# First input stage as half-product quads, and the first blocks' mixers moved beside a three-pass second input stage

## The chip, the cores and the metric

The kernel runs on one core of a Trainium2 chip, with the engines PE (matrix products), DVE (vector), ACT (scalar activation), POOL (general) and SP (which here only issues transfers). The metric is the device time of one execution in microseconds. The kernel before the change takes 2793.22 us (median of three runs, 2793.16 to 2797.24).

## The reference

One layer of an encoder on x of 2048 tokens and width 1024, in float32. The parts that matter here:

```python
xn = rms_norm(x, mix_norm_g)
proj = xn @ w_in          # q k v (512 each) | mq mk mv mo (512 each) | i f (4 each) | ga gm (1024 each)
att = chunk_band_attention(aq, ak, av, rel_bias)       # own chunk of 64 and the 8 before it, 8 heads of 64
mqk = silu(causal_depthwise_conv([mq, mk], conv_w, conv_b))            # 4 taps
hm = mlstm_chunkwise(mq_c, mk_c, mv, i, f)             # recurrence over chunks, 4 heads of 128
mlstm_out = sigmoid(mo) * rms_norm(hm, mh_norm_g)
y = sigmoid(ga) * (att @ w_att_proj) + sigmoid(gm) * (mlstm_out @ w_mlstm_proj)
x = x + y @ w_out
x = x + square(relu(rms_norm(x, ffn_norm_g) @ w_up)) @ w_down
return rms_norm(x, final_norm_g)
```

## The kernel before

**Tiles.** The tokens are cut into four blocks of 512; two blocks form a *span* (blocks 0 and 1, blocks 2 and 3). Every float32 operand of a large product is split into a high and a low part (`split`: a cast on ACT, the difference on DVE), and each product of tiles is three matmuls of 128x512: high by high, high by low, low by high. Weights arrive as raw 128x1024 tiles in four buffers `wraw`, are split into three buffers `wsp`, and one such tile feeds 24 matmuls in most stages. The operands live in 28 buffers `r` of 128x2x512. There are 16 buffers `ctx` and 6 `tmp` for 128x512 results, and 8 PSUM banks.

**Half-product quads.** A *quad* (`quad`, L594) multiplies both blocks of a span at once with 256 columns of the output, split in halves of the inner dimension, with seven products in the place of eight, from sums of quadrants of weights and of operands. It costs 7 weight tiles, 168 matmuls. The sums of x (`take_parts`, L1769) give 28 split operands. The sums of weights are made either beside an earlier stage and kept in DRAM (`sum_w`, L400; `wsum`), or when the quad loads its four raw quadrants (`quad_w`, L476). Seven products make four results; `combine` (L1829) copies three of them out of PSUM on ACT (L1840) and adds others on DVE (L1848), for each of two column groups: six copies and six sums a quad. `quad_tok` (L623) does the same for v and mv of the far span.

**The order of stages** is the body of `dense` (L677), the one thread that uses weights, in the order that `weights` (L344) lists them:

1. For block 0 and then block 1: v and mv as token tiles (`token_tiles`), 20 *feature tiles* (`feature_tile`, L535: q, k, mq, mk, mo) and 8 for the gate ga. They are plain products, 24 matmuls each. q and k go from PSUM straight into head operands (`evac_q`, `evac_k`), mq and mk through the convolution (`evac_conv`), and the block's mixers, attention (`attention`, `head`) and recurrence (`recurrence`, `rec_head`), run beside them and leave eight `r` buffers `mix`. Then the two mixer projections of the block, 16 `pair_tile` column groups, go to DRAM (`projd`).
2. The gate stage: two quads for gm of the first span; `after_gate` reads the projections back, applies the gates and writes y. Then two quads of the output projection (`after_out`).
3. The second input stage: 11 items (`IN_ORDER`: nine quads, and v/mv twice) for blocks 2 and 3. Everything is kept in DRAM.
4. Eight up-projection quads of the first span; then the down projection with the mixers of blocks 2 and 3 beside it, their inputs read from DRAM (`attention_far`, `recurrence_far`) and their projections (`project`, L799) at fixed places (`PROJ`).
5. Output, up and down of the second span, and the final norm.

**What sets the order.** `Flow` (L96) runs all threads against written-out costs of each engine and of SP, and issues each instruction on the engine that is free first, by priority; `dense` has the lowest claim on PE but its work is always there. The result is a fixed order of instructions on every engine and of transfers on SP's queue. An engine, and the SP queue, executes its list in order and stops at a wait.

## Time and profile before

| | |
|---|---|
| median of 3 runs | 2793.22 us |
| profiled execution, span from first to last instruction (no other time of it is on record) | 2794.2 us |
| PE busy | 2772.3 us (99%) |
| weight loads of PE (beside PE) | 2300.6 us (82%) |
| DVE busy | 2067.3 us (74%) |
| ACT busy | 1560.8 us (56%) |
| POOL busy | 50.4 us (2%) |
| moved by DMA | 619.31 MB, 222 GB/s over the span |
| mean granted PE clock | 0.999 |

"Busy" is the union of an engine's instructions. Matmuls overlap in the pipeline: the mean duration of one is 390 ns, while one starts every 227 ns or so, and short waits between them are hidden in "busy". The DMA share is the mean busy share of the core's 16 DMA engines. In a group's row stand the line and engine, output and inputs by the program's names, the shape, the count, busy time and mean of one, and then the idle time of the engine just before, with what ended it. The line numbers are those of the kernel before; the changed kernel's lines differ.

### The profile page before, as it was taken

How to read it: one execution, taken by the hardware profiler on the slowest of the kernel's cores; microseconds unless marked ns; L12 is line 12 of the kernel's file. 1: busy time of each engine (PE TensorE's matmuls, PEld its weight loads, DVE VectorE, ACT ScalarE, POOL GpSimd, SP SyncE). 2: the span in 40 equal slices, each digit the busy share in tenths (PEclk: the TensorE clock that was granted, in tenths of full speed). 3: DMA queues.
4: the chain of work that ended last, by engine and by line, in shares of the span. 5: the costliest groups of instructions: out<-in, count | busy, mean ns of one | idle time of the engine just before them, and what ended most of it. 6: DMA issues, size and time to landing. Idle time of an engine off the chain costs nothing.

```text
span 2794.2 us, 38148 instructions
## 1 busy us (share of the span) xinstructions
PE 2772.3 (99%) x13084; PEld 2300.6 (82%) x13084; DVE 2067.3 (74%) x3724; ACT 1560.8 (56%) x2707; POOL 50.4 (2%) x116
## 2 busy tenths in 40 slices
PE   9999999999999999999999999999999999999998
PEld 7888888888878888878888888888888888888887
DVE  7886489968995876876776788789886554457675
ACT  5674366845453544585555677476544665555453
POOL 0000000000000000000000000000000000000000
PEclk9999999999999999999999999999999999999999
DMA  6326743366845798667888876867777575678773
GB/s 223 103 90 198 275 145 97 118 200 230 265 168 198 237 314 283 210 197 261 304 298 281 273 237 209 258 210 226 233 267 232 170 259 203 210 266 274 271 246 129
DMA packets 283921, 619.31 MB, mean 222 GB/s; under 512 B 31568, under 2 KB 46544, under 8 KB 283728
## 3 DMA queue, kind: packets, MB, share of 16 engines
q1 hardware_dynamic: 283584, 616.88, 66.5%
q8 instruction: 102, 1.67, 0.2%
q14 instruction: 91, 0.75, 0.1%
q10 hardware_dynamic: 144, 0.01, 0.0%
HBM read 437.46 MB, written 179.31 MB: 221 GB/s over the span
## 4 chain that ended last, share of the span: by engine, by line
PE 84%; DVE 7%; DMA 3%; issue 3%; ACT 2%; POOL 0%; SPq 0%; POOLq 0%; ACTq 0%; DVEq 0%
PE bank L616 36%; PE bank L532 12%; PE bank L531 12%; PE bank L533 12%; PE bank L644 3%; PE bank L1272 2%; PE bank L1310 2%; PE bank L1341 2%; DVE wsp L472 2%; DMA r<-u 1%; ACT wsp L470 1%; DVE sc L1316 1%; DVE r L1020 1%; PE bank L1636 0%; DMA ctx<-x 0%
## 5 line engine op out<-in xcount | busy, mean ns | idle before, releaser
L616 PE MATMUL bank<-r,wsp 128*128 128x512 f32 x5208 | 1188.2, 390 | 2.2 <-DVE r L1020 1.0
L616 PEld LDWEIGHTS bank<-r,wsp 128*128 128x128 f32 x5208 | 976.3, 188 | 209.7 <-DVE r L1020 2.0
L472 DVE TENSOR_TENSOR wsp<-wraw,wsp 128x1024 fp32r<-128x1024 f32 x460 | 561.9, 1222 | 312.8 <-ACT wsp L470 308.6
L470 ACT CAST wsp<-wraw 128x1024 fp32r<-128x1024 f32 x460 | 483.7, 1052 | 502.5 <-PE bank L616 236.1
L531 PE MATMUL bank<-r,wsp 128*128 128x512 f32 x1600 | 635.4, 397 | 0.6 <-ACT r L1292 0.5
L532 PE MATMUL bank<-r,wsp 128*128 128x512 f32 x1600 | 624.8, 391 | 0.2 <-DVE r L1294 0.2
L533 PE MATMUL bank<-r,wsp 128*128 128x512 f32 x1600 | 624.4, 390 | 0.0
L533 PEld LDWEIGHTS bank<-r,wsp 128*128 128x128 f32 x1600 | 300.4, 188 | 64.3
L531 PEld LDWEIGHTS bank<-r,wsp 128*128 128x128 f32 x1600 | 300.7, 188 | 57.8 <-ACT r L1292 1.3
L532 PEld LDWEIGHTS bank<-r,wsp 128*128 128x128 f32 x1600 | 301.0, 188 | 55.6 <-DVE r L1294 0.8
L1020 DVE TENSOR_TENSOR r<-r 128x512 fp32r<-128x512 f32 x224 | 147.9, 686 | 60.9 <-ACT r L1015 60.1
L1848 DVE TENSOR_TENSOR ctx<-bank,ctx 128x512 f32<-128x512 f32 x174 | 119.1, 688 | 98.3 <-PE bank L616 97.8
L1015 ACT CAST r<-r 128x512 fp32r<-128x512 f32 x224 | 134.4, 622 | 91.1 <-DMA r<-u 88.6
L1840 ACT COPY ctx<-bank 128x512 f32<-128x512 f32 x174 | 100.9, 582 | 74.0 <-PE bank L616 65.7
L1322 ACT ACTIVATE sc<-sc,scs 128x640 f32<-128x640 f32 (+4 forms) x128 | 97.5, 762 | 59.6 <-DVE scs L1316 58.0
L2200 ACT ACTIVATE ctx<-ctx 128x512 f32<-128x512 f32 x96 | 60.6, 632 | 82.8 <-DVE ctx L1848 82.8
L1346 DVE TENSOR_TENSOR r<-bank,r 128x512 fp32r<-128x512 f32 (+1 forms) x168 | 98.0, 594 | 5.3 <-ACT r L1344 3.8
L1272 PE MATMUL bank<-r,r 128*128 128x512 f32 x336 | 96.8, 370 | 2.2 <-DVE r L1346 1.4
L1344 ACT CAST r<-bank 128x512 fp32r<-128x512 f32 (+1 forms) x168 | 81.8, 515 | 18.6 <-PE bank L1341 17.7
L1310 PE MATMUL bank<-r,r 128*128 128x320 f32 (+3 forms) x480 | 85.6, 305 | 0.1
L1341 PE MATMUL bank<-const,sc 128*128 128x128 f32 x560 | 80.1, 273 | 4.7 <-DVE sc L1327 2.0
L415 DVE TENSOR_TENSOR ctx<-ctx,ctx 128x512 f32<-128x512 f32 x112 | 76.3, 686 | 11.1 <-DMA wsum<-ctx 9.6
(285 smaller groups left out, 2898.7 us busy)
## 6 DMA issues: line engine op xcount, KB each, us to landing
wraw<-in_wf SPq DMA_DIRECT2D x170, 512.0 KB, 4.3
wraw<-wsum SPq DMA_DIRECT2D x136, 512.0 KB, 4.2
r<-u SPq DMA_DIRECT2D x224, 256.0 KB, 4.5
wraw<-in_w SPq DMA_DIRECT2D x103, 512.0 KB, 3.6
u<-ctx SPq DMA_DIRECT2D x128, 256.0 KB, 2.4
ctx<-in_wf SPq DMA_DIRECT2D x112, 256.0 KB, 4.1
wsum<-ctx SPq DMA_DIRECT2D x112, 256.0 KB, 3.6
u<-tmp SPq DMA_DIRECT2D x96, 256.0 KB, 3.3
```

The lines of the kernel that those rows point to most:

```text
L470: nc.scalar.copy(w[:, 0], raw)
L472: nc.vector.tensor_sub(w[:, 1], raw, w[:, 0].bitcast(F32))
L531: mm(ps, lh, rh, start=first, stop=False)
L532: mm(ps, lh, rl, start=False, stop=False)
L533: mm(ps, ll, rh, start=False, stop=last)
L616: mm(ps, wv[:, x, k, n], a[:, y], start=new and k == 0 and x == y == 0, stop=k == 3 and x == 1, skip_group_check=True)
L1015: self.nc.scalar.copy(dst[:, 0], src)
L1020: self.nc.vector.tensor_sub(dst[:, 1], src, dst[:, 0].bitcast(F32))
L1272: nc.tensor.matmul(bkv[:, :, c0:c0 + w], st, sl[:, :, o:o + w], start=n == 0, stop=n == total - 1)
L1310: nc.tensor.matmul(bks[x][:, :w], q[:, y, i * P:(i + 1) * P], kf[:, f * P + x * w:f * P + x * w + w], start=y == 0, stop=y == 1)
L1341: nc.tensor.transpose(bk[:, o:o + P], prob[i][0][:, c:c + P], self.ident)
L1848: nc.vector.tensor_add(t[:, o:o + 512], ps, t[:, o:o + 512])
```

## The change

Five things change together.

- **First input stage.** The feature tiles, the gate stage and its two quads go. `dense` first runs v and mv of blocks 0 and 1 as token tiles, and then nine quads (`IN_FIRST`: gm0, q, mq, ga0, k, mk, gm1, mo, ga1) for blocks 0 and 1, from the summed x of both. Their results go to DRAM in the form that blocks 2 and 3 already had. `norm_in` of block 1 runs beside that of block 0.
- **Sums of the second span's x.** They are made beside the first stage and kept in DRAM (`take_x1`, `xud`): 28 tiles.
- **Second input stage in three passes** (`in_far`, `BATCHES`): pass one takes products 0, 3, 1 of all 11 items, pass two 2 and 4, pass three 5 and 6, so that 12 or 8 operands are in use and not 28. A ring of 16 `r` buffers holds them. Partial sums are *parked*: pass one stores one tile per item and column group, pass two loads it, finishes one result and stores another sum, pass three loads both and finishes two results.
- **Mixers of blocks 0 and 1** run beside these passes, from DRAM, with the code that blocks 2 and 3 used; all mixers write their output to DRAM (`mixd`, `keep_mix`), and `load_mix` reads it back before `project`. Projection of block 0 stands in pass two ahead of item 6, that of block 1 in pass three ahead of item 5.
- **Weights.** Nine quads of the first stage come with their sums made on load (but the first), and these are kept for the second stage; one more sum is made beside other work (15 for 14).

```diff
+IN_FIRST = ("gm0", "q", "mq", "ga0", "k", "mk", "gm1", "mo", "ga1")
 IN_ORDER = ("gm0", "gm1", "q", "mq", "vm0", "ga0", "k", "vm1", "mk", "ga1", "mo")
+BATCHES = ((0, 3, 1), (2, 4), (5, 6))
+PROJ_IN = {(1, 6): 0, (2, 5): 1}
...
+    def in_far(self, A, aev, ring):
...
+        self.banks.want = 4
+        for g, batch in enumerate(BATCHES):
...
+            room = Pool([0] * (4 + 2 * g))
+            if g > 0:
+                fl.spawn(self.unpark(g, kept, got, gev, room), 1)
+            if g == 1:
+                self.load_mix(0, ring)
+            for i, name in enumerate(IN_ORDER):
+                self.sum_at(g + 1, i)
+                if (g, i) in PROJ_IN:
+                    b = PROJ_IN[g, i]
+                    yield from self.project(b, ring)
+                    if b == 0:
+                        fl.spawn(self.take_batch(BATCHES[2], A, aev, ring), 1)
+                        self.load_mix(1, ring)
...
+                yield from self.product(p, batch[0], A, aev, bank, None, release)
+                if g == 0:
...
+                        fl.spawn(self.park_first(n, t, tev[n], bank[n], clear[n], o), 1)
+                    yield from self.product(p, batch[1], A, aev, other, None, release)
...
+                        fl.spawn(self.park_u2(i, n, t, tev[n], other[n], kept[i][0][n], o), 1)
+                    yield from self.product(p, batch[2], A, aev, bank, clear, release)
...
+    def park_v(self, i, n, got, gev, ps, clear, kept, o):
+        yield "wait", [gev[0][n]]
+        (t,) = yield "get", self.ctx, 1
+        yield "dve!", dve_ns(512)
+        self.nc.vector.tensor_add(t[:, :512], ps, got[0][n][:, o:o + 512])
+        self.fl.set(clear)
+        yield from self.store(self.parkd.ap()[i, 1, n], t[:, :512], kept, self.ctx, t)
...
+    def finish_far(self, finish, n, which, x, got, gev, ps, clear, o, room):
+        yield "wait", [gev[x][n]]
+        t = got[x][n]
+        yield "dve!", dve_ns(512)
+        self.nc.vector.tensor_add(t[:, o:o + 512], ps, t[:, o:o + 512])
...
     def dense(self):
...
         for b in range(2):
             B = self.blk[b]
...
+            yield from self.token_tiles(B["xg"], B["xn"], lambda t, bk, b=b: self.evac_v(b, t, bk))
...
+            yield from self.token_tiles(B["xg"], B["xn"], lambda t, bk, b=b: self.evac_mv(b, t, bk), True)
...
-            for j in range(4):
-                for fn in (self.evac_q, self.evac_k, self.evac_conv_q, self.evac_conv_k, self.evac_og):
-                    (bk,) = yield from self.feature_tile(xs, none if b > 0 or j > 0 else B["xs_done"])
...
-            for j in range(8):
-                (bk,) = yield from self.feature_tile(xs, none)
-                fl.spawn(self.evac_ga(b, j, bk), 1)
...
-            yield from self.quad(*G, self.after_gate(i, O), release=i == N_G - 1)
...
+        for i, name in enumerate(IN_FIRST):
...
+            if last:
+                fl.spawn(self.reserve(ring, N_IN), 0)
+                fl.spawn(self.take_batches(X1, ring), 0)
+                self.mixers(0)
+            yield from self.quad(*X, self.combine(self.after_in(0, name), off(name)), release=last)
+        yield from self.in_far(*X1, ring)
```

More of the change, by code (lines that the diff above doesn't have):

```diff
@@ L234, in dve2_ns, with off @@
     return 70 + 0.55 * n
+def off(name):
+    return 3 if name in ("mq", "mk") else 0
 class Layer:
@@ new lines, in take_batches, with take_batch, reserve @@
+    def take_batches(self, X, ring):
+        for batch in BATCHES[:2]:
+            yield from self.take_batch(batch, *X, ring)
+    def take_batch(self, batch, A, aev, ring):
+        fl = self.fl
+        for m in batch:
+            for k in range(4):
+                yield "wait", [self.xu_ev[m][k]]
+                (r,) = yield "get", ring, 1
+                A[m][k] = r
+                fl.spawn(self.take_u1(self.xud.ap()[m, k], r, aev[m][k]), 0)
+    def reserve(self, room, n, after=()):
+        yield "wait", list(after)
+        for _ in range(n):
+            self.fl.put(room, *(yield "get", self.rpool, 1))
@@ L652, in down @@
+    def down(self, s, m, ring, A, aev, blocks, room):
         fl = self.fl
@@ L1594, in evac_og @@
[L1594 to L1605 removed]
+        fl = self.fl
@@ L1797, in take_parts @@
         if k > 1:
-            yield "wait", [aev[m][k - 2] for m in range(7)]
-        pool = (self.ctx, self.temp)[k % 2 if scale == 1.0 else 0]
+            yield "wait", [evs[m][k - 2] for m in range(7)]
+        pool = pool or (self.ctx, self.temp)[k % 2 if scale == 1.0 else 0]
         got = yield "get", pool, 5
@@ L1803, in take_parts @@
             yield from load(b, j, a)
-        if read is not None:
-            self.fl.set(read)
+        if read is not None and not ahead:
+            fl.set(read)
         done = []
@@ L2081, in after_out @@
         fl.spawn(load(), 1)
-        for n in range(2 if s > 0 and q > 0 else 0):
+        for n in range(2 if q > 0 else 0):
             fl.spawn(self.spread(ht[n], hev[n], 2 * q + n, U), 1)
```

1048 lines of the change are left out of this document (414 added, 634 removed).

## The prediction

> **What bounds the kernel now.** I read the engine shares first, then PE in stretches, then PE's waits, then the DMA share.
>
> ```profile
> span 2794.2 us, 38148 instructions
> PE 2772.3 (99%) x13084; PEld 2300.6 (82%) x13084; DVE 2067.3 (74%) x3724; ACT 1560.8 (56%) x2707; POOL 50.4 (2%) x116
> q1 hardware_dynamic: 283584, 616.88, 66.5%
> PE 84%; DVE 7%; DMA 3%; issue 3%; ACT 2%; POOL 0%; SPq 0%; POOLq 0%; ACTq 0%; DVEq 0%
> ```
>
> PE is busy for all but 21.9 us, and the chain that ended last runs 84% through it. The stretches (PE, PEld, DVE, ACT, POOL busy; clock; DMA share; GB/s) show where it loses anything:
>
> ```profile
> 0.00:50.00 50.00, 48.36 (x224) 39.10 (x225) 35.95 (x78) 27.18 (x41) 2.84 (x13) 1.00 0.76 262
> 1600.00:1800.00 200.00, 197.59 (x1045) 165.01 (x1044) 172.14 (x433) 122.83 (x267) 7.20 (x22) 1.00 0.76 233
> 1800.00:2000.00 200.00, 199.43 (x1071) 169.91 (x1069) 179.20 (x420) 138.30 (x287) 4.88 (x16) 1.00 0.70 215
> 2200.00:2400.00 200.00, 200.00 (x880) 164.92 (x879) 105.43 (x131) 114.10 (x167) 0.00 (x0) 1.00 0.65 221
> 2600.00:2794.00 194.00, 184.97 (x856) 153.96 (x854) 123.95 (x171) 83.05 (x119) 3.02 (x3) 0.99 0.61 209
> ```
>
> 9.0 us of that lie in the last row, which the change leaves alone. The row 2200:2400 holds 512-column matmuls alone: 200 us / 880 = 227.3 ns each. This, and not the mean of 390 ns in the groups, is the price of a matmul, because neighbours overlap. In the rows 1600:2000 two blocks' mixers run beside the down projection with DVE 86 to 90% busy, and PE loses 3.0 us in 400. PE is the bound, at full clock.
>
> **The change, part by part.**
>
> ```profile
> L616 PE MATMUL bank<-r,wsp 128*128 128x512 f32 x5208 | 1188.2, 390 | 2.2 <-DVE r L1020 1.0
> L531 PE MATMUL bank<-r,wsp 128*128 128x512 f32 x1600 | 635.4, 397 | 0.6 <-ACT r L1292 0.5
> L644 PE MATMUL bank<-wsp,r 128*128 128x512 f32 x336 | 77.0, 390 | 0.8 <-DVE ctx L1848 0.8
> ```
>
> 1. *Fewer products.* Blocks 0 and 1 had 28 feature tiles each of 24 matmuls (1344) and two gate quads of 168 (336). Nine quads of 7 products x 24 = 1512 take the place of these 1680. The instruction lists of both kernels confirm it: 10728 matmuls of a weight tile before (5208 and 336 in the rows, 3 x 1600 in the row of L531 and its two neighbours, 3 x 128 in pair form), 10560 after; the rest of PE's list has equal counts. 168 x 227.3 ns = **-38.2 us**, all on the path. Bounds: 38.1 us by the closest spacing of a long row (1330:1400 below, 70 us / 309), and 40 if short waits stood between the saved ones; the 397 ns of the row L531 would give 67, but its matmuls overlap.
>
> [...]
>
> 2. *Combining.* The second input stage (nine quads and v/mv, 11 items) used six DVE sums and six ACT copies an item, now ten sums and two copies, since partial sums are parked: 22 first sums, 22 second, 66 finishing.
>
> ```profile
> L472 DVE TENSOR_TENSOR wsp<-wraw,wsp 128x1024 fp32r<-128x1024 f32 x460 | 561.9, 1222 | 312.8 <-ACT wsp L470 308.6
> L1848 DVE TENSOR_TENSOR ctx<-bank,ctx 128x512 f32<-128x512 f32 x174 | 119.1, 688 | 98.3 <-PE bank L616 97.8
> L1840 ACT COPY ctx<-bank 128x512 f32<-128x512 f32 x174 | 100.9, 582 | 74.0 <-PE bank L616 65.7
> L1294 DVE TENSOR_TENSOR r<-tmp,r 64x256 fp32r<-64x256 f32 x64 | 26.7, 417 | 2.1 <-ACT r L1292 0.9
> ```
>
> ```profile
> L1174 DVE TENSOR_TENSOR r<-bank,r 64x512 fp32r<-64x512 f32 x16 | 11.0, 690 | 2.1 <-ACT r L1172 1.7
> L1157 DVE SCALAR_TENSOR_TENSOR r<-bank,r 64x512 fp32r<-64x512 f32 x16 | 11.0, 686 | 0.6 <-ACT r L1155 0.2
> L1160 DVE CAST r<-r 64x512 fp32r<-64x512 f32 x16 | 6.7, 421 | 0.5
> ```
>
> DVE gets 260 such sums for 174, +86 x 0.688 = +59 us, and loses the splits of L1294 (-27), the near q and k evictions (-29), seven splits of weight tiles (L472, 460 to 453, -9) and smaller things of the gate stage and the near norm. Its list has 3686 instructions for 3726; ACT's 2431 for 2502, with the output gate's scaling moved there from POOL. Both stay near 2067 and 1561 us in total, beside PE: 0 on the path. If the cover fails, DVE is where it shows: summing its list at the rows' means, from the start of the second input stage to the end of block 0's projection, gives 403 us beside some 420 of PE, the density of the rows 1600:2000 (447 beside 460 by the same sum), which cost 3 us in 400.
>
> 3. *The new wait.* In passes two and three a finishing sum on DVE needs its parked tile back from DRAM. DVE works in order, so the low halves of the next weight tiles queue behind it, and PE behind those; PE also waits for the bank. Six to eight tiles may be fetched ahead, two or four used per 10.9 us of PE (48 matmuls), so the fetch leads by 20 to 30 us. Like loads land in 4 to 5 us:
>
> ```profile
> r<-u SPq DMA_DIRECT2D x224, 256.0 KB, 4.5
> r<-qfar SPq DMA_DIRECT2D x32, 256.0 KB, 5.7
> tmp<-proj SPq DMA_DIRECT2D x32, 256.0 KB, 4.2
> ```
>
> ```profile
> L2184 SPq DMA_DIRECT2D r<-u x224: 319/370/1821, 1497.1 to 2736.2; - x112
> ```
>
> The last row gives what one order holds SP's queue (shortest, median, longest, in ns).
>
> So 0, while the DMA engines keep up. Whether they do is the open term.
>
> 4. *DMA.* Gone: the 64 transfers of projections, 32 of normalised x, kept k and half of v's. New: 44 stores and 66 loads of parked sums, 28 and 28 of x sums, 112 loads of k for 48 and 64 of q for 32, gates 64 and 64 for 32 and 32, mixer outputs 80 stores and 32 loads. Sums: 2416 issues for 1918, 734.9 MB for 616.8. SP gives one order in 0.32 to 0.37 us, 0.9 ms for all, so its queue is not the limit. By stretch, bytes against PE's time matter. Between the first weight tile of the second input stage and the first of the up projection the new list moves 225.1 MB: weights 63.4, parked sums 28.8, mixers' inputs 34, weight sums 22, gates 18.6, the rest stage results. PE in it: 1848 + 384 + 336 = 2568 matmuls x 0.2273 = 584 us, and two blocks' mixers. All else on PE is 2772.3 - 10728 x 0.2273 = 334 us for four blocks with rows, tail and short waits, so two mixers are under 167; I take 145. That is 729 us and 309 GB/s. What the engines can do:
>
> ```profile
> 10.00:20.00 10.00, 9.95 (x44) 7.92 (x43) 9.93 (x18) 8.82 (x14) 0.00 (x0) 1.00 1.00 332
> 1330.00:1400.00 70.00, 70.00 (x309) 57.61 (x308) 48.70 (x62) 39.91 (x60) 0.00 (x0) 1.00 0.85 303
> 1500.00:1520.00 20.00, 20.00 (x90) 16.38 (x89) 13.54 (x17) 13.87 (x26) 0.00 (x0) 1.00 0.99 348
> 1500.00:1550.00 50.00, 50.00 (x240) 41.76 (x239) 29.18 (x40) 27.80 (x49) 0.05 (x1) 1.00 0.98 329
> 1600.00:1650.00 50.00, 48.01 (x265) 40.35 (x264) 41.80 (x108) 33.46 (x74) 2.31 (x8) 1.00 0.80 236
> 1650.00:1700.00 50.00, 50.00 (x273) 42.73 (x272) 48.15 (x112) 35.14 (x76) 2.04 (x6) 1.00 0.79 236
> ```
>
> Full share is worth 332 GB/s (also the page's mean: 616.88 MB in 66.5% of 2794.2 us), but only 295 to 299 beside mixers (236 / 0.80, 236 / 0.79), whose lines are short. 113 MB of the 225 fall beside mixers: 113 / 0.297 + 112 / 0.332 = 380 + 337 = 717 us of full DMA work in 729 us of PE. For 50 us a share of 0.98 cost PE nothing; over 700 us every order of SP that waits for a buffer or a result loses some. Ends: 0 (0.98 throughout), and at 0.90, 717 / 0.90 - 729 = +68 us. I take 0.96, just under the 0.98 that held for 50 us, as the stretch is 14 times as long: 717 / 0.96 = 747, **+18 us**. What would be late are weight tiles and parked tiles.
>
> [...]
>
> ```profile
> 5.48 1.20 PE L531 MATMUL bank<-wsp,r 128*128 128x512 f32 x4 [0.65 <-ACT wsp L453]
> ```
>
> 5. *Start.* Sixteen token tiles (87 us) now come before the first quad, eight (44 us) before the first feature until now. In that time DMA must bring x of both blocks twice and store v. 32.2 MB of SP's list end with the last x row that the first quad's third product needs. At the 262 GB/s of the row 0:50 that is 123 us, at 332 97 us, and PE would be there at about 107 us (5.5 us to the first weight matmul, the row above, 384 x 0.2273, the row broadcasts, two products of 5.5 us). PE's list lets half of the third and fourth product and the gate matmuls, some 10 us, go ahead of the late rows. So between 0 and 16 us; I take **+3**, nearer to the cover.
>
> 6. *Order.* Gate stage, its 32 loads and its tanh go; nothing waited for them last (the waits of PE name none). Projections 0 and 1 now read mixers back from DRAM, but both blocks' mixers are done in PE's list where projection 0 begins, so 0. Blocks 2 and 3 keep their place beside the first down projection; their outputs also go through DRAM now, at some 260 GB/s of demand in that stretch, less than the row 1330:1400 bore. The tail is unchanged.
>
> Sum against the profiled execution: 2794.2 - 38.2 + 18 + 3 = 2777 us; its span is 1.0 us above the median of the runs, 2793.22. **Forecast 2776 us.**
>
> **The rivals.**
> A. *DMA hidden throughout.* For it: 70 us at 303 GB/s and 50 at 329 with PE full. Against: ten times as long. 2793.2 - 38.2 + 3 = 2758, so 2755 to 2762. [...]
> B. *DMA is the bound of the second input stage, and the kernel is slower.* It decides from where the saving is used up: 729 + 35 = 764 us for the 717 of work, a mean share of 0.94. At 0.90: 2793 - 38 + 68 + 3 = 2826. For it: the rows beside mixers, and the SP queue, which stops at every store that waits for DVE. Against: SP stops less when transfers are already late.
> C. *Loss and gain cancel*, share 0.932 to 0.945: 2788 to 2798.
> That the products are not saved is excluded by the lists.
>
> **How the numbers follow.** A measurement tells 0.2% (5.6 us). Forecast case (2763 to 2787) 0.38, A 0.30, C 0.13, B 0.19. So faster 0.68, same 0.13, slower 0.19. The range reaches from A's floor, 2754, into B as far as 2808 (share 0.92), leaving about 0.15 out; the faster cases alone span 2754 to 2787.
>
> **What would show it.** Step 1: 168 fewer matmuls, the big ones still at 227 ns in the second up projection. Steps 2 and 3: in PE's waits, finishing sums or weight tiles named for more than a few us would prove me wrong. Step 4: DMA share 0.95 or more from about 450 to 1180 us, PE idle there some 20 us, landing times above 5 us. Step 5: PE idle between 90 and 130 us. What would make it wrong: it fails most easily if that long stretch runs at a share below 0.94, or if PE stays full at 0.98.

## The result and the profile after

The changed kernel takes 2812.36 us (median of 4 runs, 2811.32 to 2813.18) beside 2794.20 us for the kernel before on the same chip (4 runs, 2793.16 to 2797.24): ratio 1.0064, 95% interval 1.0050 to 1.0078. The profiled execution took 2812.02 us. The kernel is slower, by about 18 us (0.6%), where 17 us less were forecast, and it ends 4 us above the range's upper end.

From the page of the kernel after (span, engines, DMA queue, chain that ended last):

```profile
span 2810.2 us, 38516 instructions
PE 2752.5 (98%) x12916; PEld 2280.1 (81%) x12916; DVE 2053.5 (73%) x3684; ACT 1538.8 (55%) x2636; POOL 37.6 (1%) x108
q1 hardware_dynamic: 353060, 735.04, 77.7%
PE 80%; DVE 7%; DMA 6%; issue 3%; ACT 2%; SPq 1%; POOL 0%; POOLq 0%; ACTq 0%; DVEq 0%
```

PE has 168 matmuls fewer, as planned, and is busy 19.8 us less, but it idles 57.7 us where it idled 21.9. Its share of the chain falls from 84 to 80%, and DMA gains three points: transfers that the chain had to wait for.

The stretches of the kernel after (PE, PEld, DVE, ACT, POOL busy; granted clock; DMA share; GB/s). The first four answer to stretches shown of before:

```profile
0.00:50.00 50.00, 47.90 (x208) 40.30 (x209) 37.39 (x71) 33.30 (x53) 1.59 (x5) 0.97 0.86 291
1600.00:1800.00 200.00, 189.92 (x1024) 159.66 (x1023) 167.47 (x434) 129.23 (x277) 7.15 (x24) 0.99 0.81 254
1800.00:2000.00 200.00, 198.80 (x1045) 169.29 (x1045) 169.19 (x388) 128.31 (x252) 4.77 (x15) 1.00 0.76 237
2200.00:2400.00 200.00, 200.00 (x880) 164.94 (x879) 102.80 (x125) 114.46 (x168) 0.00 (x0) 1.00 0.62 215
400.00:600.00 200.00, 181.21 (x909) 149.37 (x908) 138.84 (x361) 114.29 (x260) 7.01 (x25) 0.93 0.87 280
600.00:900.00 300.00, 298.53 (x1548) 252.57 (x1547) 244.74 (x556) 183.08 (x365) 6.71 (x23) 1.00 0.85 279
900.00:1200.00 300.00, 286.20 (x1236) 230.01 (x1235) 221.29 (x317) 127.64 (x174) 0.00 (x0) 0.99 0.92 313
410.00:1190.00 780.00, 745.94 (x3601) 615.38 (x3600) 597.22 (x1223) 415.70 (x788) 13.72 (x48) 0.98 0.88 291
```

The last of them in the kernel before:

```profile
410.00:1190.00 780.00, 777.69 (x3610) 643.64 (x3610) 623.23 (x1022) 415.07 (x701) 12.68 (x19) 1.00 0.63 209
```

The row 2200:2400 is the same as before, 880 matmuls in 200 us. Apart from the start and the end, PE stands still in three places: 18.8 us at 400 to 600 us, where the second input stage and the first blocks' mixers begin; 13.8 us at 900 to 1200 us, the last passes and the output quads; and 10.1 us at 1600 to 1800 us, where the mixers of blocks 2 and 3 run beside the down projection (2.4 us before).

Idle time leaves out short waits between overlapping matmuls and matmuls at a lower clock. So the losses below are counted otherwise: for every two successive starts on PE, the distance less the median distance of that kind of matmul (line and width), where that is positive. This is called *excess* here. It is read from the profiled execution of each kernel, which took within 5 us of the median, but 9 us less than it in `el_poolq`. In us:

| stretch, us | before | after | difference |
|---|---|---|---|
| 0 to 400 | 16.0 | 7.1 | -8.9 |
| 400 to 600 | 6.5 | 35.1 | +28.6 |
| 600 to 900 | 2.9 | 9.1 | +6.2 |
| 900 to 1200 | 1.3 | 20.8 | +19.5 |
| 1500 to 1850 | 15.0 | 26.4 | +11.4 |
| the rest | 13.0 | 9.6 | -3.4 |
| sum | 54.7 | 108.2 | +53.5 |

With the 38.2 us saved, 53.5 - 38.2 = +15.3 us, and the spans differ by 16.0. So the saving is there in full, and what took it is these waits.

**400 to 600 us.** The timeline of PE in the kernel after (start, length, what ended the idle time before):

```profile
464.91 0.49 PE L1539 MATMUL bank<-cst,r 128*128 128x129 f32 x2
468.03 0.69 PE L1260 MATMUL bank<-r,r 128*128 128x128 f32 x2 [2.63 <-DMA r<-kfar]
469.86 1.12 PE L1573 MATMUL bank<-const,ctx 128*128 128x128 f32 x4 [1.14 <-DVE ctx L1563]
479.19 1.12 PE L1512 MATMUL bank<-const,r 128*128 128x128 f32 x4 [8.22 <-DMA r<-mfar]
493.77 0.80 PE L654 MATMUL bank<-r,wsp 128*128 128x512 f32 x1 [0.28 <-ACT r L1079]
```

and SP's orders in the same time:

```profile
474.22 0.59 SPq L1477 DMA_DIRECT2D r<-mfar  x1
474.85 0.43 SPq L1615 DMA_DIRECT2D tmp<-in_xt  x1
478.65 0.84 SPq L1615 DMA_DIRECT2D tmp<-in_xt  x2
484.63 0.43 SPq L1957 DMA_DIRECT2D xu<-tmp  x1
488.66 0.40 SPq L2011 DMA_DIRECT2D r<-xu  x1
```

From 464.5 to 493.8 us PE has no product of weights to do. The next one (L654) needs the last of four groups of normalised x sums of span 1 (`take_x1`), whose rows are only ordered at 474.9 to 479 us, whose sums are stored from 484.6 us on and come back from 488.7 us on. In the meantime only a few mixer matmuls are in the list, and these wait for their own inputs.

**900 to 1200 us.** DVE's and PE's waits from 950 to 1200 us in the kernel after (total, times, longest):

```profile
DVE ctx L776 <- DMA ctx<-park: 18.5, 8, 4.6
DVE tmp L964 <- DMA tmp<-gate: 14.8, 8, 3.0
```

```profile
PE bank L659 <- DVE ctx L776: 5.2, 1, 5.2
PE bank L654 <- DVE ctx L776: 4.6, 5, 1.4
```

L776 is the finishing sum. It waits for its parked tile, and PE for its bank. The gates that come back from DRAM are late too (L964). Pairing each order of a parked tile with the sum that uses it gives the lead: for the 22 loads of the second pass 20 to 99 us to the finishing sum, and 11 to 94 us to the sum that reads the tile first (L751); but 4 to 8 us for 18 of the next 20, which is hardly more than the 4.7 us (median) that such a load takes to land. For the last 24 it is 5 to 46 us.

**1700 to 1850 us.** From 1742.0 to 1764.2 us PE's list holds no matmul of the down projection; the kernel before had no such gap of over 4 us beside these mixers. ACT's waits from 1700 to 1800 us begin with

```profile
ACT r L1079 <- DMA r<-mix: 10.0, 2, 8.9
```

a mixer output on its way back from DRAM, with splits of weight tiles behind it.

### The profile page after: what moved, and what is told of

Read it like the earlier page. It is cut to its first block, busy times and chain, and to the rows that moved or that the text cites. A ratio compares the mean times of both kernels' runs of the same rounds, so it can differ in the third digit from the quotient of the medians.

```text
span 2810.2 us, 38516 instructions
## 1 busy us (share of the span) xinstructions
PE 2752.5 (98%) x12916; PEld 2280.1 (81%) x12916; DVE 2053.5 (73%) x3684; ACT 1538.8 (55%) x2636; POOL 37.6 (1%) x108
## 4 chain that ended last, share of the span: by engine, by line
PE 80%; DVE 7%; DMA 6%; issue 3%; ACT 2%; SPq 1%; POOL 0%; POOLq 0%; ACTq 0%; DVEq 0%
PE bank L623 38%; PE bank L554 8%; PE bank L555 8%; PE bank L556 8%; PE bank L654 8%; PE bank L1218 2%; PE bank L1291 2%; DVE wsp L495 2%; PE bank L659 2%; PE bank L1260 2%; DMA ctx<-park 1%; DMA r<-u 1%; DMA r<-mix 1%; ACT wsp L493 1%; DVE sc L1266 1%
## 5 line engine op out<-in xcount | busy, mean ns | idle before, releaser
L623 PE MATMUL bank<-r,wsp 128*128 128x512 f32 x4872 | 1114.5, 390 | 2.7 <-ACT r L1081 1.0
L623 PEld LDWEIGHTS bank<-r,wsp 128*128 128x128 f32 x4872 | 912.8, 188 | 198.3 <-issue 1.9
L493 ACT CAST wsp<-wraw 128x1024 fp32r<-128x1024 f32 x453 | 475.9, 1051 | 525.0 <-PE bank L623 221.2
L495 DVE TENSOR_TENSOR wsp<-wraw,wsp 128x1024 fp32r<-128x1024 f32 x453 | 552.7, 1220 | 287.3 <-ACT wsp L493 275.8
L554 PE MATMUL bank<-r,wsp 128*128 128x512 f32 x1152 | 454.8, 395 | 2.3 <-ACT r L1079 1.7
L555 PE MATMUL bank<-r,wsp 128*128 128x512 f32 x1152 | 449.5, 390 | 0.0
L556 PE MATMUL bank<-r,wsp 128*128 128x512 f32 x1152 | 448.9, 390 | 0.0
L654 PE MATMUL bank<-r,wsp 128*128 128x512 f32 x1512 | 373.3, 395 | 5.3 <-DVE ctx L776 4.6
L654 PEld LDWEIGHTS bank<-r,wsp 128*128 128x128 f32 x1512 | 278.8, 189 | 62.9 <-DVE ctx L776 3.5
L556 PEld LDWEIGHTS bank<-r,wsp 128*128 128x128 f32 x1152 | 216.3, 188 | 45.8
L554 PEld LDWEIGHTS bank<-r,wsp 128*128 128x128 f32 x1152 | 216.4, 188 | 44.4 <-ACT r L1079 2.1
L555 PEld LDWEIGHTS bank<-r,wsp 128*128 128x128 f32 x1152 | 216.6, 188 | 40.6 <-DVE r L1084 0.2
L1079 ACT CAST r<-r 128x512 fp32r<-128x512 f32 x284 | 171.7, 621 | 121.2 <-DMA r<-u 89.9
L1084 DVE TENSOR_TENSOR r<-r 128x512 fp32r<-128x512 f32 x284 | 188.8, 685 | 65.0 <-ACT r L1079 64.2
L1711 DVE TENSOR_TENSOR ctx<-bank,ctx 128x512 f32<-128x512 f32 x150 | 103.1, 688 | 96.5 <-PE bank L623 96.0
L1703 ACT COPY ctx<-bank 128x512 f32<-128x512 f32 x150 | 87.0, 581 | 56.9 <-PE bank L623 55.9
L1296 DVE TENSOR_TENSOR r<-bank,r 128x512 fp32r<-128x512 f32 (+1 forms) x168 | 95.8, 592 | 11.7 <-ACT r L1294 11.1
```

Of the source, the lines that this page charges most:

```text
L493: nc.scalar.copy(w[:, 0], raw)
L495: nc.vector.tensor_sub(w[:, 1], raw, w[:, 0].bitcast(F32))
L554: mm(ps, lh, rh, start=first, stop=False)
L555: mm(ps, lh, rl, start=False, stop=False)
L556: mm(ps, ll, rh, start=False, stop=last)
L623: mm(ps, wv[:, x, k, n], a[:, y], start=new and k == 0 and x == y == 0, stop=k == 3 and x == 1, skip_group_check=True)
```

## The experiments

Times are medians; the kernel before took 2794.0 to 2796.2 us beside them. A ratio is to the kernel before.

### The start of the second input stage: early_x, late_mix, early_late

`early_x`:

```
-            if i == 5:
+            if i == 3:
                 ready, read = Event(), [Event() for _ in range(4)]
                 fl.spawn(self.rows_far(1, ready, read), 2)
```

`late_mix` (`early_late` has both):

```
             if last:
...
-                self.mixers(0)
...
     def in_far(self, A, aev, ring):
...
                 self.sum_at(g + 1, i)
+                if (g, i) == (0, 1):
+                    self.mixers(0)
```

> The normalised x sums of span 1 (four groups k of four x rows, seven sums each, kept in DRAM) are begun at the fourth quad of the first input stage instead of the sixth; nothing else is changed. Theory 'late operands' (PE's 15.7 us of idle time at 450 to 500 us, with the clock fallen to 0.76, is the wait for the fourth group, whose rows were ordered only at 474.9 to 479.2 us): the fourth group is stored before the last quad ends, PE idles under 4 us between 440 and 520 us, the excess of 25 us there falls to some 5, and the kernel takes 2788 to 2797 us. Rival 'DMA is full' (its share is 0.9 to 1.06 from 440 to 485 us, and the same bytes have to move): PE still loses 12 us or more around the start of the second input stage, or loses them in the first stage instead, and the time stays within 2806 to 2818 us.

> The mixers of blocks 0 and 1 are begun one item later (with the second item of the second input stage, some 33 us of PE later) instead of with the last quad of the first stage. Theory 'late operands, because the mixers' loads and temp tiles get in between': the fourth group of x sums is no longer held up, PE idles under 4 us at 440 to 520 us, and 2788 to 2798 us come out unless the mixers then end too late for projection 0 (that would show as a wait of PE ahead of the projection). Rival 'DMA is full whatever starts then': the idle time stays at 12 us or more, time 2806 to 2818 us. Rival 'the x sums are late by themselves' (one group after the other, five temp tiles each): some of the wait stays, 5 to 12 us, with no mixer in it, time 2798 to 2808 us.

> Both edits together: the x sums of span 1 from the fourth quad on, and the mixers of blocks 0 and 1 with the second item of the second input stage. One at a time they took 6.8 and 12.4 us off 2812.4, and each left a wait: the recurrence for a rotated output, and the third product for the last x sums. Theory 'late operands': the two waits are independent, both go, PE idles under 4 us at 440 to 540 us, the excess at 400 to 600 us falls from 35 to under 12 us, and the time is 2786 to 2796 us. Rival 'DMA is full there': the losses of the two edits don't add up; 2796 to 2806 us, with idle time moved to 500 to 700 us.

| kernel | time | ratio, 95% interval | excess 400-600 | 600-900 | 900-1200 | sum |
|---|---|---|---|---|---|---|
| after | 2812.4 | 1.0064 (1.0050 to 1.0078) | 35.1 | 9.1 | 20.8 | 65.0 |
| early_x | 2805.6 | 1.0041 (1.0026 to 1.0056) | 19.4 | 8.6 | 27.1 | 55.1 |
| late_mix | 2800.0 | 1.0018 (1.0008 to 1.0027) | 20.6 | 19.5 | 14.6 | 54.7 |
| early_late | 2805.8 | 1.0043 (1.0028 to 1.0058) | 10.1 | 19.9 | 27.3 | 57.3 |

The wait at 480 us is a matter of order: each edit takes 15 us of the excess at 400 to 600 us, both together 25. The time follows only in part. `late_mix` comes out as its second rival had it, that the x sums are late by themselves: one wait of PE for their last group is left (7.9 us), and no mixer is in it. `early_x` ends just under its rival's range and far from its theory's. In `early_late` 17 of the 25 us are lost again at 600 to 1200 us, and the sum over the stage stays at 55 to 57 us in all three. The rival of `early_late` came true in time. In place it did not: the excess at 500 to 700 us is 12.0 us, for 13.8 in the kernel after, and the loss went to 700 to 900 us (16.0 for 5.2) and 900 to 1200 us.

### The parked tiles: park_memset, sums_away, sum_sc, early_late_sc

`park_memset`, `sums_away` and `sum_sc`, in this order:

```
-                    yield "sp", 900, 2000
-                    self.nc.sync.dma_start(t[:, o:o + 512], self.parkd.ap()[i, x, n])
+                    yield "pool", 600
+                    self.nc.gpsimd.memset(t[:, o:o + 512], 0.0)
...
-... enumerate(((1, 2), (1, 7), (2, 2), (4, 0), (4, 1), (4, 2), (4, 3), (4, 4)))})
+... enumerate(tuple((4, i) for i in range(8)))})
...
-            got = yield "get", self.ctx, 4
+            pool = self.sc if q == SUMS[2, 2] else self.ctx
+            got = yield "get", pool, 4
...
```

> The 66 loads of parked sums (17.3 MB) are left out: the tiles are set to zero by POOL instead, so the output of the blocks 2 and 3 is wrong by the parked part; their stores, ctx tiles and DVE sums stay. Theory 'the wait for parked tiles is what costs PE at 950 to 1200 us': the finishing sums no longer wait, PE idles under 4 us there, time 2798 to 2804 us, the loss at 450 to 500 us unchanged. Rival 'the DMA engines are the bound and weight tiles are late too': also some gain, since 17.3 MB are gone, but then PE's waits at 950 to 1200 us would go over to weight tiles and gates, with 5 us or more left. Rival 'POOL's writes slow DVE, or ctx tiles are the real shortage': no gain, 2808 us or more.

> The three sums of down weights that are made beside the second input stage (at 693 to 1033 us; each takes four of the 16 ctx tiles twice and moves 4.2 MB) are made beside the first up projection with the other five. Theory 'no room to fetch ahead' (parked tiles were ordered only 4 to 8 us before their use from 983 to 1042 us, because ctx tiles were short): the lead grows to 15 us or more there, the finishing sums' wait for parked tiles (18.5 us on DVE) falls under 5 us, PE's idle time at 950 to 1200 us falls from 13.4 to under 5 us, and the time to 2798 to 2805 us. Rival 'DMA engines are the bound' (share 0.91 to 0.93 there): the loss shrinks only as the bytes do (8 of some 114 MB after 800 us), by 2 to 5 us, with the lead still short, and part of it comes back in the up projection, which gets 12.6 MB more (85 MB in 307 us before): 2806 to 2812 us.

> The third sum of down weights beside the second input stage takes the four sc tiles, which only mixers and square sums use, in place of four ctx tiles; every transfer and every byte stays. Theory 'ctx tiles short, so no room to fetch parked tiles ahead': the lead of the parked tiles at 983 to 1042 us grows from 4 to 8 us to 15 us or more, the excess at 900 to 1200 us falls from 20.9 to 8 to 13 us (8.7 with the sums away, 11.2 with the loads left out), time 2800 to 2806 us. Rival 'the bytes are the bound' (share 0.92): the excess stays at 17 us or more, time 2809 to 2814 us.

> The edits of the two runs before together. If the causes are separate, the gains add: 2812.4 less some 20 for the start of the second input stage and some 8 for the parked tiles, 2778 to 2789 us, which is below the 2795 of the kernel before. If the DMA engines set the pace of the second input stage as a whole (the 225 MB at a share near 0.93), the gains don't add and the time stays at 2792 us or more.

Without the loads of parked tiles 2801.0 us come out (1.0026, 1.0016 to 1.0036), in the range of the theory of the wait for them, though 5.4 us of idle time stay at 950 to 1200 us where it allowed 4. The excess at 900 to 1200 us falls from 20.8 to 11.3: about half of that loss goes with these loads. Whether by the wait for them or by their 17.3 MB, this run does not tell, since it leaves out both. With the sums away it falls to 8.7, and the lead of the first twenty tiles of the third pass, most of which had 4 to 8 us, grows to 16 to 36 us. But the time is 2836.9 us (1.0148, 1.0131 to 1.0165), with the sums now reaching into the mixers of blocks 2 and 3: the excess at 1700 to 1850 us is 56.8 us, for 16.2.

`sum_sc` was to tell whether ctx tiles or transfers were short. It frees the four ctx tiles of the third sum and keeps every transfer: the lead stays at 4 to 9 us for 18 of the twenty, and the time is 2809.9 us (1.0063, 1.0047 to 1.0080), where the ctx theory had 2800 to 2806. So these four tiles are not what keeps the lead short. That SP's list, with all its transfers, ran late is what is left, and it is argued, not shown. (The excess at 900 to 1200 us did fall to 14.2, between the two theories, which the lead does not explain; the profiled execution was 5 us faster than the median.) `early_late_sc` stays at 2804.4 us (1.0035, 1.0022 to 1.0048), so the gains do not add.

### Whether transfers set the pace: el_memset, el_twice, el_poolq, land45

`el_memset` is `early_late` with the memset above. `el_twice` and `el_poolq` change `early_late` so:

```
                     self.nc.sync.dma_start(t[:, o:o + 512], self.parkd.ap()[i, x, n])
+                    yield "sp", 900, 2000
+                    self.nc.sync.dma_start(t[:, o:o + 512], self.parkd.ap()[i, x, n])
...
     def store(self, dst, src, ev, pool=None, item=None, queue="sp"):
-        yield queue, 900, 2000
-        self.nc.sync.dma_start(dst, src)
+        yield "pool", 1100, 2000
+        self.nc.gpsimd.dma_start(dst, src)
```

`land45` changes each `yield "sp", 900, 2000` of the kernel after to `900, 4500` (and 1750, 2000 to 1750, 4500).

> The two early and late edits (x sums of span 1 from the fourth quad, mixers of blocks 0 and 1 an item later), and the 66 loads of parked sums left out (POOL zeroes the tiles; the outputs of blocks 2 and 3 are wrong by the parked part). Up to now every rearrangement left PE's excess at 400 to 1200 us where it was (65 us after, 55 to 61 in five rearranged kernels), only in other places. Theory 'the second input stage is held by the rate at which transfers get through': 17.3 MB less, worth 17.3/0.295 = 59 us of it, take away most of the excess: under 30 us at 400 to 1200, time 2765 to 2782 us. Rival 'order and ctx tiles': the parked loads being gone mends 900 to 1200 alone (27 to some 12 us), what went over to 600 to 900 stays (20 us); excess about 42 us, 2785 to 2795 us.

> The two early and late edits, and each parked tile loaded twice, one load after the other: 17.3 MB and 66 orders more, no other work. Theory 'rate of transfers': the loss at 700 to 1200 us grows by a good part of 17.3/0.295 = 59 us, 2830 to 2870 us. Rival 'order and ctx tiles': the extra load lengthens the time from order to use by some 5 us where the lead is short (22 tiles), so 2812 to 2828 us; if neither counts, 2804 to 2810 us.

> The two early and late edits, and all stores that go through the common store routine (results, parked sums, x sums, gates; not weight sums of quads and not mixer outputs' own helper) are ordered by POOL in place of SP, so that a store which waits for its data no longer holds up the loads behind it. SP stood waiting for 418 of 780 us at 420 to 1200 us, of which stores hold about a half. Theory 'SP's single queue is what keeps the engines at a share of 0.88': the share rises to 0.92 or more where PE waits, excess at 400 to 1200 us falls from 57 to under 35 us, 2775 to 2792 us. Rival 'the engines themselves': no gain, 2800 to 2812 us. Rival 'POOL's orders cost more': POOL's orders take over 1 us each and slow the stores and DVE; 2812 us or more.

> The kernel after, with one number of its planner changed: it plans 4.5 us from an order of SP to the landing, as the rows of transfers have it, where it planned 2.0 us. No work is added or removed, only the order of the instructions moves. Theory 'instructions stand too early in the in-order lists for data that comes through DRAM' (parked tiles, mixer outputs, x sums): the waits of PE and ACT for loads shrink in all three places, excess 108 to under 90 us, time 2785 to 2803 us. Rival 'buffers, not the order, are short': the planner holds the same tiles for longer and fetches later; no gain or a loss, 2809 to 2830 us.

| kernel | time | ratio, 95% interval | excess 400-600 | 600-900 | 900-1200 | sum |
|---|---|---|---|---|---|---|
| early_late | 2805.8 | 1.0043 (1.0028 to 1.0058) | 10.1 | 19.9 | 27.3 | 57.3 |
| el_memset | 2783.7 | 0.9960 (0.9946 to 0.9974) | 9.8 | 17.9 | 9.9 | 37.6 |
| el_twice | 2866.9 | 1.0258 (1.0242 to 1.0273) | 11.7 | 18.1 | 91.5 | 121.3 |
| el_poolq | 2838.2 | 1.0150 (1.0133 to 1.0166) | 16.2 | 24.9 | 15.8 | 56.9 |
| land45 | 2886.4 | 1.0337 (1.0321 to 1.0353) | 40.2 | 7.6 | 30.4 | 78.2 |

The stretch 900 to 1200 us of `early_late`, `el_memset` and `el_twice`, in this order:

```profile
900.00:1200.00 300.00, 285.42 (x1207) 229.34 (x1206) 221.74 (x318) 128.79 (x176) 0.00 (x0) 0.97 0.91 310
```

```profile
900.00:1200.00 300.00, 295.07 (x1284) 240.94 (x1283) 233.28 (x336) 140.63 (x196) 23.95 (x46) 0.99 0.81 272
```

```profile
900.00:1200.00 300.00, 237.21 (x923) 183.07 (x922) 187.79 (x273) 96.78 (x134) 0.00 (x0) 0.90 0.89 298
```

The 17.3 MB and 66 orders of the parked loads cost 22 us, nearly all of it at 900 to 1200 us. The result lies between the theories: the rate of transfers asked for under 30 us of excess and 2765 to 2782 us, the rival for about 42 us and 2785 to 2795. It is nearer to the rival, which has the place right as well: the 18 us at 600 to 900 us, where some of the 66 loads fall, hardly move.

`el_twice` lands in the range of the rate of transfers (2830 to 2870 us), but it answers less than was meant. The expectation missed that the second load into a tile waits on SP for the first one to land. SP's waits in `el_twice` at 420 to 1200 us and PE's at 900 to 1200 us:

```profile
SPq L769 <- DMA ctx<-park: 54.4, 36, 4.2
```

```profile
PE bank L654 <- DVE ctx L780: 39.3, 14, 8.8
PE bank L659 <- DVE ctx L780: 8.0, 2, 6.1
```

SP stands 54.4 us for the second orders, but not longer in sum: all its waits from 420 to 1200 us add up to 413 us, beside 418 in `early_late`, 419 in the kernel after, and 562 in the kernel before, which has an excess of 10.7 us in that stretch. Nor do the engines move more: from 410 to 1190 us it is 292 GB/s at a share of 0.89, beside 294 GB/s at 0.89 in `early_late`. PE stands still 63 of the 300 us at 900 to 1200 us. The kernel is 61 us longer, and 17.3 MB take 59 us at 292 GB/s; but 54.4 us of waits in the order of the queue cost about as much. The run fits both.

Taking the stores off SP's queue (`el_poolq`) does lower the excess at 900 to 1200 us, 27.3 to 15.8, but with the stores on POOL's queue the excess rises elsewhere, by 11 us each at 0 to 400 and 400 to 900 us, and by 7 at 1200 to 1500 us, and the time is in the range of the third rival, that POOL's orders cost more. But the page has 541 ns of POOL for an order, not over 1 us (mean of the 128 `u<-ctx` stores; SP gave them in 320 ns, median, in the kernel after), so the cause is not shown. These three runs do not separate the rate of the DMA engines from the in-order queue.

`land45` falls outside both ranges, on the side of its rival: planning with the measured time to landing makes the kernel 74 us slower, with the loss at 1700 to 2100 us (78.5 us for 21.0). The cause stays open; that the planner then holds buffers for longer is only argued.

### The weight sums in the first stage: front3, front3_proj, front3_proj9, front3_early, front4_proj

`front3` is `early_late` with the three sums in the first input stage:

```
-... enumerate(((1, 2), (1, 7), (2, 2), (4, 0), ...
+... enumerate(((9, 0), (9, 1), (9, 2), (4, 0), ...
...
     def sum_at(self, stage, i):
...
+        if stage == 0 and i in (2, 4, 6):
+            self.fl.spawn(self.sum_w(SUMS[9, (2, 4, 6).index(i)], sc=True), 3)
...
```

The others add to it: `PROJ_IN = {(1, 7): 0, (2, 6): 1}` (`front3_proj`) or `{(1, 9): 0, (2, 6): 1}` (`front3_proj9`); the mixers at their old place (`front3_early`, original `PROJ_IN`); a fourth sum, at `i` = 7 (`front4_proj`, with the places of `front3_proj`).

> The two early and late edits, and the three sums of down weights leave the second input stage for the first (where the DMA share was 0.67 to 0.79 at 100 to 350 us): they are made there in the four sc tiles, beside the others. Theory 'bytes of the second input stage': 12.6 MB fewer in it are worth up to 40 us of transfers; the excess at 400 to 1200 us falls from 57 to 30 us or less, 2772 to 2786 us. Rival 'order and ctx tiles': the lead of the parked tiles grows and 900 to 1200 us falls from 27 to about 10 us, the 30 us before it stay; 2786 to 2794 us. Rival 'the first stage is as sensitive' : what is won is lost there, 2800 us or more.

> As the run before, and projections 0 and 1 come one item later (before items 7 and 6 of the second and third pass, instead of 6 and 5). Theory 'projection 0 waits for the mixers, which were begun an item later': the waits of attention's and recurrence's matmuls at 750 to 850 us (5 us named, clock 0.93, excess of about 16 us) go, the excess at 600 to 900 us falls to under 11 us, 8 to 10 us below the run before. Rival 'only DMA': no difference, within 4 us of the run before.

> The late start of the mixers is kept, with the early x sums and the three weight sums in the first stage, and projection 0 comes before item 9 of the second pass instead of item 6, projection 1 before item 6 of the third. Theory 'PE waits at projection 0 for the mixers': the excess at 600 to 900 us falls from 26 (31 with one item) to under 14 us, 2778 to 2790 us. Rival 'the rate of transfers sets the sum over the stage, and one item later changed it by 1 us only': 2790 to 2797 us.

> The x sums of span 1 from the fourth quad on and the three weight sums in the first stage on sc tiles, but the mixers of blocks 0 and 1 begin with the last quad, as in the kernel after. Theory 'the late start of the mixers is what costs 600 to 900 us': the excess there falls from 26 to 9 to 12 us, 400 to 600 us takes 12 to 19 us (8.6 with the late start), 900 to 1200 us 13 to 19 us; 2784 to 2794 us. Rival 'the rate of transfers sets the sum over the stage': 400 to 1200 us keeps some 50 to 55 us of excess, 2794 to 2800 us.

> As the run before, and a fourth sum of down weights leaves the first up projection for the first input stage, so that the last of them ends before the mixers of blocks 2 and 3 begin. Theory 'the last sum, at 1480 to 1644 us, holds ctx tiles that these mixers and the returned mixer outputs need': the excess at 1500 to 1850 us falls from 27 to under 18 us (15 before), 8 us or more below the run before. Rival 'that loss has nothing to do with sums': no difference there, and 4.2 MB more in the early stages cost 0 to 10 us.

| kernel | time | ratio, 95% interval | excess 400-600 | 600-900 | 900-1200 | sum |
|---|---|---|---|---|---|---|
| front3 | 2797.5 | 1.0010 (1.0000 to 1.0019) | 8.6 | 25.7 | 19.3 | 53.6 |
| front3_proj | 2794.0 | 0.9995 (0.9986 to 1.0004) | 6.2 | 30.9 | 13.2 | 50.3 |
| front3_proj9 | 2791.6 | 0.9992 (0.9983 to 1.0000) | 9.5 | 27.5 | 10.4 | 47.4 |
| front3_early | 2810.1 | 1.0056 (1.0043 to 1.0070) | 18.7 | 24.1 | 20.0 | 62.8 |
| front4_proj | 2820.8 | 1.0094 (1.0078 to 1.0110) | 7.5 | 51.9 | 14.5 | 73.9 |

`front3` was to take 12.6 MB, 48 transfers, out of the second input stage, whose first product starts at 456 us. The transfers of these sums from 440 to 1190 us, `early_late` first:

```profile
wsum<-ctx SPq DMA_DIRECT2D x42, 256.0 KB, 4.0
ctx<-in_wf SPq DMA_DIRECT2D x40, 256.0 KB, 4.9
```

```profile
wsum<-ctx SPq DMA_DIRECT2D x24, 256.0 KB, 4.9
ctx<-in_wf SPq DMA_DIRECT2D x20, 256.0 KB, 5.0
wsum<-sc SPq DMA_DIRECT2D x12, 256.0 KB, 5.4
sc<-in_wf SPq DMA_DIRECT2D x8, 256.0 KB, 5.1
```

These are 82 and 64, so only 18 transfers, 4.7 MB, left the stage: the third of the moved sums, and more of the first stage's own than before, now stand at its beginning. The time falls by 8 us, and all three theories missed. With the projections later the kernel is as fast as the one before the change, which fits the rivals of `front3_proj` and `front3_proj9`; the latter is at best 0.2% faster, within what can be told. Neither theory for 600 to 900 us holds: the 24 to 31 us there stay with the mixers begun at the old place and with projection 0 three items later, and both forecasts for `front3_early` were too low. In `front4_proj` PE runs nothing but mixers from 776.8 to 827.1 us; the excess at 1500 to 1850 us falls by 4 us only, so the last sum is not what costs there, and the kernel loses 27 us, where the rival allowed 10.

The bytes alone do not set these losses. Summed over 400 to 1200 us, the excess falls by 4 us for 4.7 MB less (`front3`), by 12 us for 12.6 MB less (`sums_away`) and by 11 and 20 us for 17.3 MB less (`park_memset`, `el_memset`), and rises by 64 us for 17.3 MB more (`el_twice`). At the 295 GB/s of the expectations these bytes would be 16, 43, 59 and 59 us.

### Projection 2: mix_land, proj2_late

```
-        yield from self.take_u1(self.mixd.ap()[b, x], r, B["mixed"][x])
+        yield from self.take_u1(self.mixd.ap()[b, x], r, B["mixed"][x], 8000)
...
-PROJ = {2: (3, 0), 3: (6, 0)}
+PROJ = {2: (3, 2), 3: (6, 0)}
```

> The kernel after, and the planner takes 8.0 us instead of 2.0 from the order to the landing of a mixer output that comes back from DRAM, so that its split on ACT stands later in ACT's list; nothing else is changed. ACT waited 8.9 us for such a tile at 1768 to 1777 us, and weight tiles stood behind it. Theory 'the split of the returned mixer output stands too early': the excess at 1700 to 1850 us falls from 16.2 to 7 to 10 us (6.9 before), time 2803 to 2808 us. Rival 'the mixers' own chains are what PE waits for there' (attention's and recurrence's rows name 5 us of the waits): the excess stays at 14 us or more and the time at 2809 to 2815 us.

> The kernel after with projection 2 half a product group later (before the third instead of the first pair of weight tiles of the fourth group of the first down projection). From 1740.7 to 1763.3 us no down matmul ran on PE, only the mixers' own, with their waits; before had no such gap. Theory 'PE's list waits there for projection 2's operands, which come later since the mixer outputs go through DRAM': the gap closes and the excess at 1700 to 1850 us falls from 16.2 to 6 to 10 us, time 2802 to 2807 us. Rival 'DVE and ACT are what is full there': the excess stays at 14 us or more, 2809 to 2815 us.

`mix_land` is slower, 2823.0 us (1.0104, 1.0086 to 1.0122), with 18.9 us of excess at 1700 to 1850 us: the early split on ACT is not the cause by itself. `proj2_late` closes the gap of 22 us and lowers that excess from 16.2 to 12.6, but another gap without a down matmul opens from 2004.8 to 2024.0 us, and 13.6 us more are lost at 1850 to 2100 us; 2827.2 us (1.0114, 1.0097 to 1.0131). No forecast of the time held in these two runs. Projection 2's wait is a part of the loss at most, and the rest stays open.

## Why the prediction was wrong

1. *Fewer products, -38.2 us:* right. 13084 - 12916 = 168 matmuls, the long row unchanged at 227.3 ns, and the balance of excess and saving meets the span within 1 us.
2. *Combining, 0:* right as far as the traces show. DVE's total went from 2067.3 to 2053.5 us and ACT's from 1560.8 to 1538.8. DVE was 69 to 82% busy in the three stretches of 400 to 1200 us, and where PE waited most for DVE at 950 to 1200 us, it was for sums that themselves waited for a load.
3. *The new wait, 0 "while the DMA engines keep up":* this step failed. The fetch was to lead by 20 to 30 us. It did in the second pass and not in the third, where it led by 4 to 8 us; removing the loads of the parked tiles is worth 11 us in the kernel after and 22 us in `early_late`. The room of eight tiles, from which the step worked out its lead, did not give it. What held the orders back is not shown; four more free ctx tiles did not lengthen the lead (`sum_sc`).
4. *DMA, +18 us:* the right direction and too small; this term, with step 6, turned the sign. The excess from 400 to 1200 us grew by 54.3 us (28.6 + 6.2 + 19.5). The mean share was 0.88, not 0.96, and so under the 0.94 from which the step itself made the kernel slower. Its price for transfers beside mixers was too high: 279 GB/s at 0.85 (600 to 900 us) is 328 GB/s at full share, where 295 to 299 were taken, and the whole stretch gives 291 / 0.88 = 331. Nor is it shown that the short lines, which the step names there, lowered the rate: in the kernel before, 38% of the packets are under 2 KB at 1500 to 1550 us, with 329 / 0.98 = 336 GB/s, and 33% at 1600 to 1700 us, with 295 to 299. With both numbers put right the step's own sum would have been 225.1 / 0.331 / 0.88 - 729 = +44 us. The choice of 0.96 "just under the 0.98 that held for 50 us" was the error: the row of 50 us did not carry over to 780 us. Landing times above 5 us, the sign that the step named, showed for some transfers only: in the median 4.7 us for the parked loads and 5.6 us for the gates that come back at 950 to 1200 us. How much of the 54.3 us is this term and how much is order (step 6) stays open.
5. *Start, +3 us:* not seen. No wait of more than 0.3 us showed between 85 and 135 us, and the excess at 0 to 400 us, which holds more than the start, fell from 16.0 to 7.1.
6. *Order, 0:* failed at two places it did not price. The start of the second input stage was not in the list of steps at all: 28.6 us (a part of the 54.3 above), of which the two edits of order remove 25, though the time gains only 7 (12 with `late_mix` alone). And blocks 2 and 3 lost 11.4 us beside the down projection, where "less than the row 1330:1400 bore" looked at GB/s and not at the chain store, load, split, projection; what that chain costs is shown only in part.

Of the rivals, B named the side, with 2826 us at a share of 0.90; the measured 2812 lies between it and C. At the measured share of 0.88 its own sum would give 2844 us: it shares step 4's price per byte, which was too high. The SP queue does stop at stores that wait for DVE (102 of its 419 us of waits from 420 to 1200 us stand at the store routine, for DVE), but that these stops set the pace, as its mechanism had it, is not shown. A was wrong.

What stays open: the 37 to 47 us of excess at 400 to 1200 us that no edit removed, above all the 18 to 31 us at 600 to 900 us in the kernels with the late start of the mixers or the moved sums (52 in `front4_proj`), and whether the DMA engines or SP's in-order queue holds them.

## What to carry to other kernels

A stage that runs for hundreds of us at a high DMA share is not nearly free because a row of 50 us was: here 50 us at 0.98 had cost PE nothing, and a stage of 780 us at 0.88 went with 54.3 us more of excess, part of it a matter of order. When several edits move a loss without shrinking its sum over the stage, look for what the whole stage is short of; here leaving out the loads of parked tiles shrank it most, and what holds the rest is open. The sum of the ordering queue's waits does not tell: it was larger in the kernel before (562 us, and 419 after). Check a fetch ahead by pairing order and use in the trace, as a count of buffers (eight here) did not tell its lead (20 to 30 us by the count, 4 to 8 in the third pass). And check in the trace that an edit moved what it was to move: of the 48 transfers that `front3` was to move out of the stage, 18 went.

## What the runs showed of the hardware

PE's clock fell with the idle time at 470 us and made it dearer. The kernel after, in stretches of 5 us (columns as above):

```profile
465.00:470.00 5.00, 1.23 (x6) 0.85 (x6) 2.56 (x11) 2.20 (x9) 1.01 (x1) 0.76 0.88 284
470.00:475.00 5.00, 0.97 (x4) 0.57 (x4) 0.69 (x1) 0.00 (x0) 0.00 (x0) 0.50 1.04 308
475.00:480.00 5.00, 0.81 (x4) 0.71 (x4) 0.14 (x1) 0.00 (x0) 0.00 (x0) 0.50 1.06 323
480.00:485.00 5.00, 4.29 (x20) 3.72 (x19) 3.40 (x5) 1.14 (x4) 0.00 (x0) 0.53 1.06 362
485.00:490.00 5.00, 3.72 (x26) 3.10 (x26) 4.97 (x14) 2.77 (x13) 0.29 (x2) 1.00 0.79 229
```

The granted clock is 0.50 from 470 to 480 us and still 0.53 while PE works again up to 485 us. In stretches of 1 us it is 1.00 up to 467 us, 0.81 in the next and 0.50 from 468 us on, where PE has run nothing from 465.4 to 468.0 us. It is back at 1.00 from 485 us on, after some 5 us in which PE was mostly busy (4.29 of the 5 us from 480). At the low clock the same work takes longer: from the start of a pair of L1538 to the next start, a pair of L1539, it is 0.43 us at 484.1 us and 0.22 us at 460.1 us. It is one reason why the excess of a stretch is larger than its idle time (35.1 beside 18.8 us).

In these rows the DMA share is over 1.00 for 15 us, with up to 362 GB/s. From 410 to 1190 us `early_late` keeps 294 GB/s at 0.89, and `el_twice`, with 17.3 MB more to load, 292 GB/s at 0.89. Whether 0.89 is the most that this mix of loads and stores gets for long, or what the waits in SP's list leave, these runs do not tell.
